# A three-stage transformer block on one NeuronCore: another product order and pinned transposes in the down projections

## The chip, the cores and the metric

The kernel runs on one NeuronCore of a Trainium2 chip. Its engines work side by side, each through its own list of instructions in order: PE (TensorE, matrix products and transposes), ACT (ScalarE), DVE (VectorE), POOL (GpSimd) and SP (SyncE, which here only issues DMAs). The metric is the device time of one execution in microseconds (us); lower is better.

## The reference

The layer has 1024 tokens of width 1024 and everything is float32:

```
x  = LN1(alpha*x + 0.5*SwiGLU_1(x))             # d_ff = 2816
x  = LN2(alpha*x + mixer(x))                    # GLA heads, and indexer -> top-256 keys -> attention
x  = LN3(alpha*x + 0.5*SwiGLU_2(x))
SwiGLU(x) = (silu(x @ Wg) * (x @ Wu)) @ Wd
LN(x) = (x - mean) * rsqrt(var + 1e-5) * g + b  # over the 1024 columns of a token
```

The mixer begins with one projection of x: a narrow one, m (the index key and gates, 112 columns), the four index queries iq (128 columns each), and then keys, values and the rest.

## The kernel before, in words

Every float32 product is made of three matmuls on pairs of fp32r tiles, a high part (`xh`, `whid`: a copy by ACT) and the rest (`xl`, `wlod`: a subtraction by DVE, L93 or L182).

A feed-forward stage is a "gate and up" part followed by `down`, here called Down 1 and Down 2. `down` multiplies 1024 x 2816 by 2816 x 1024 as seven half-size products (the scheme of Strassen in Winograd's form), in the order of the table `DOWN`: A11, A12, S4, S1, S2, S3, A22. Each product sums eleven tiles i = 0..10 into four PSUM banks `pd`, twelve matmuls a tile (L471), 132 a product; the last one adds to blocks 4 to 7. A tile is loaded by SP (`rd`, a half from `h_dram` and a half from the weights or their sums `t_dram`, L461 and L462) into a ring, and split by ACT (`whid`, L92) and DVE (`wlod`, L93). The results are added to eight blocks `acc` of 128 tokens each (L501 to L514), through the middle sum `u`, which is first the A11 product and becomes A11 + S2 (L506). Since S2 is the fifth product, the second halves of blocks 0 to 3 and both halves of blocks 4 to 7 get their part of `u` only then (L507, L518 and the next).

A block that is complete gets its layer norm: statistics (L207, L209, L211), POOL's power of -0.5 (`rs`, L193), then for most blocks DVE's `nb` (L221), ACT's scaling (L222), POOL's multiplication by g (L223) and DVE's addition of b (L224). Only blocks 4 to 7 of Down 2 take the other branch, `last`, on DVE alone (L215 over 1024 columns, L218 twice over 512). Blocks 0 to 3 are normed after the fifth product, blocks 4 to 7 after the last.

Down 1's blocks are transposed for the mixer by `split_T`: eight transposes a block on PE (L180) in two PSUM tiles `tp` of four, each of which ACT copies (`xh`, L181) and DVE subtracts from (`xl`, L182). `tp` has two buffers. Blocks 0 to 3 are transposed one each after i = 3, 4, 5, 6 of the last product; in that product PE's order is pinned by `in_order`, while ACT and DVE follow the scheduler's list. Then `index_parts` makes the mixer's first projections (`proj_feat`, L607 to L609, banks `pf` of two buffers) for tokens 0 to 511: m, evicted to `ik_hi`, `ik_lo` and `mT` (L640, L643, L644), and four iq (L651, L652), with the transposes of blocks 4 to 7 between them; then the same for tokens 512 to 1023. In between stand pieces of the index scores (`ps`, L682) and of the search for the top keys, which fill DVE in the mixer.

Of the kernel before, what the change touches and what calls it, by code (L numbers as in the profile page):

```python
# [111 lines left out]
class Block:  # L112
# [26 lines left out]
    def in_order(self):  # L139
# [6 lines left out]
        prev = None  # L146
        for i in body[start:]:
            if i.engine == mybir.EngineType.PE:
                if prev is not None:
                    self.tc.add_manual_dep(  # L150
                        i,
                        prev.name,
                        mybir.DependencyInfo(mybir.DependencyClass.NoSync, mybir.DependencyReason.DATA),
                        reason="in_order",
                    )
                prev = i
# [43 lines left out]
    def layer_norm(self, t, g_bc, b_bc, scale=1.0, last=False, st=None):  # L200
# [5 lines left out]
        for c in range(1 if made else 2):  # L206
            nc.vector.bn_stats(st[:, c, :], t[:, c * 512 : (c + 1) * 512])  # L207
# [6 lines left out]
        if last:  # L214
# [25 lines left out]
    DOWN = (("A11", "11"), ("A12", "21"), ("S4", "22"), ("S1", "T1"), ("S2", "T2"), ("S3", "T3"), ("A22", "T4"))  # L240
# [200 lines left out]
    def down(self, w_down, h_dram, t_dram, ps, load, after_block, after_all=None, ordered=None):  # L441
# [7 lines left out]
        last = len(self.DOWN) - 1  # L449

# [16 lines left out]
        def add(banks, r, i, hl):  # L467
            lh, ll = [x[:, r * P : (r + 1) * P] for x in hl]
            wh, wl = [x[:, HT:] for x in hl]
            for n, (left, right) in enumerate(((lh, wh), (lh, wl), (ll, wh))):  # L470
                nc.tensor.matmul(  # L471
                    banks[r], left, right, start=(i == 0 and n == 0), stop=(i == ng - 1 and n == 2)
                )

        ends = range(ng - (4 if ordered else RING), ng)
        done = list(range(4))
        acc = None
        for m in range(last + 1):
            pools = ((ps, "z"), (ps, "y")) if m % 2 == 0 else ((self.ps_tp, "tp"), (self.ps_pj, "pj"))
            banks = [pool.tile([P, 512], F32, tag=t, name=self.uid("pd"), bufs=2) for pool, t in pools for _ in range(2)]  # L480
            if m == last and ordered:
                ordered.enter_context(self.in_order())
            for i in range(ng if m < last else ends[0]):
                hl = prepare(m, i)
                for r in range(4):
                    add(banks, r, i, hl)
                if m == 0 and i == 2:
                    acc, u = load()
                    c11, c12 = [[acc[r][:, c * 512 : (c + 1) * 512] for r in range(4)] for c in range(2)]
                    c21, c22 = [[acc[4 + r][:, c * 512 : (c + 1) * 512] for r in range(4)] for c in range(2)]  # L490
                if m == last and after_all and i >= 3:
                    after_all(done.pop(0), acc)
            if m == last:
                made = [prepare(m, i) for i in ends]
            for r in range(4):
                p = banks[r]
                if m == 0:
                    nc.scalar.activation(u[r], p, AF.Copy)
                elif m in (1, 2):
                    c = (c11, c12)[m - 1][r]  # L500
                    V.scalar_tensor_tensor(c, c, 2.0 * ALPHA, p, ALU.mult, ALU.add)  # L501
                elif m == 3:
                    V.tensor_add(c12[r], c12[r], p)
                    V.scalar_tensor_tensor(c22[r], c22[r], 2.0 * ALPHA, p, ALU.mult, ALU.add)
                elif m == 4:
                    V.tensor_add(u[r], u[r], p)  # L506
                    V.tensor_add(c12[r], c12[r], u[r])  # L507
                elif m == 5:
                    V.tensor_add(c22[r], c22[r], p)
                    V.tensor_add(c21[r], c21[r], p)  # L510
                else:
                    for i, hl in zip(ends, made):
                        add(banks, r, i, hl)
                    V.tensor_add(c21[r], c21[r], p)  # L514
                    after_block(4 + r, acc, stats[r])
            if m == 1:
                for r in range(4):
                    V.tensor_add(c11[r], c11[r], u[r])  # L518
            elif m == 4:
                for r in range(4):  # L520
                    after_block(r, acc)
                    V.tensor_add(c22[r], c22[r], u[r])
                    V.scalar_tensor_tensor(c21[r], c21[r], 2.0 * ALPHA, u[r], ALU.mult, ALU.add)
            elif m == 5:
                stats = []
                for r in range(4):
                    stats.append(self.small.tile([P, 2, 6], F32, tag="st2", name=self.uid("st"), bufs=4))
                    V.bn_stats(stats[r][:, 1, :], c22[r])
        if after_all:
            for b in done:  # L530
                after_all(b, acc)
        return [(b, acc) for b in range(4, NB)]
# [94 lines left out]
    def index_parts(self, u, xT, ip, mT, between):  # L627
# [6 lines left out]
        for i in range(2):  # L634
# [9 lines left out]
            nc.scalar.activation(mT[64 : R_GA + 16, ts], pt[64 : R_GA + 16], AF.Copy)  # L644
            for t in range(4):
# [7 lines left out]
                if i == 0 and t:  # L653
# [425 lines left out]
    def run(self):  # L1079
# [80 lines left out]
        def back(n, ps, src, norm, after_block, *more):  # L1160

            kept, st = ExitStack(), ExitStack()
            pools = [
# [357 lines left out]
```

## Time and profile before

| | |
|---|---|
| median of 3 runs | 2080.42 us (2080.06 to 2080.82) |
| profiled execution | 2082.8 us, of which span 2081.0 us |
| granted clock of PE, mean | 0.974 |
| PE, DVE, ACT, POOL busy | 96%, 72%, 40%, 28% |
| Down 1, first `pd` matmul to the mixer's first projection | 453.67 to 677.52 us |
| index projections, first half of the tokens | 677.52 to 721.28 us |
| end of the span | 2081.0 us |

The rows further down give start and length of an instruction in us from the span's start, the engine, the line, the operation, what it writes and reads, and in brackets how long the engine had been idle and for what. The length of a PE row contains its pipeline: back to back, matmuls of 512 columns start about 0.23 us apart though each shows 0.39 us. [...]

### The profile page before, as it was taken

How to read it: one execution, taken by the hardware profiler on the slowest of the kernel's cores; microseconds unless marked ns; L12 is line 12 of the kernel's file. 1: busy time of each engine (PE TensorE's matmuls, PEld its weight loads, DVE VectorE, ACT ScalarE, POOL GpSimd, SP SyncE). 2: the span in 40 equal slices, each digit the busy share in tenths (PEclk: the TensorE clock that was granted, in tenths of full speed). 3: DMA queues.
4: the chain of work that ended last, by engine and by line, in shares of the span. 5: the costliest groups of instructions: out<-in, count | busy, mean ns of one | idle time of the engine just before them, and what ended most of it. 6: DMA issues, size and time to landing. Idle time of an engine off the chain costs nothing.

```text
span 2081.0 us, 26915 instructions
## 1 busy us (share of the span) xinstructions
PE 2004.6 (96%) x9752; PEld 1627.6 (78%) x9752; DVE 1500.3 (72%) x2378; ACT 836.1 (40%) x1330; POOL 591.6 (28%) x443
## 2 busy tenths in 40 slices
PE   8999999999998899899999899999999999999997
PEld 6888888888887688677777677787888888888885
DVE  5587787775578579999966455557587787775578
ACT  4323323334334344678544344423323323334332
POOL 3344454430003202133233000026354464420003
PEclk9999999999999999898998799999999999999999
DMA  5345445478655122011227521152345454478654
GB/s 172 112 152 188 138 163 169 142 253 291 201 179 182 61 91 86 17 54 57 53 85 169 147 72 36 52 189 75 123 154 179 142 174 150 145 273 274 201 184 151
DMA packets 192709, 298.44 MB, mean 143 GB/s; under 512 B 16304, under 2 KB 98368, under 8 KB 192576
## 3 DMA queue, kind: packets, MB, share of 16 engines
q1 hardware_dynamic: 192576, 296.72, 44.1%
q8 instruction: 77, 1.26, 0.3%
q14 instruction: 56, 0.46, 0.1%
HBM read 205.96 MB, written 90.70 MB: 143 GB/s over the span
## 4 chain that ended last, share of the span: by engine, by line
PE 73%; DVE 16%; issue 4%; DMA 3%; ACT 2%; POOL 1%; SPq 0%; POOLq 0%; DVEq 0%; ACTq 0%
PE pq L305 13%; PE pq L307 13%; PE pq L306 13%; PE pd L471 13%; DVE junk L732 3%; PE pv L1062 3%; PE tpe L1050 2%; PE pf L607 2%; PE pf L608 2%; DVE wlod L93 2%; PE pf L609 2%; PE pt L620 2%; PE pt L622 1%; PE pt L621 1%; DVE score L689 1%
## 5 line engine op out<-in xcount | busy, mean ns | idle before, releaser
L93 DVE TENSOR_TENSOR wloq<-rw,whiq 128x512 fp32r<-128x512 f32 (+1 forms) x208 | 213.8, 1030 | 110.9 <-ACT whiq L92 110.4
L93 DVE TENSOR_TENSOR wlod<-rd,whid 128x1024 fp32r<-128x1024 f32 x154 | 189.2, 1235 | 132.4 <-ACT whid L92 131.4
L92 ACT ACTIVATE whid<-rd 128x1024 fp32r<-128x1024 f32 x154 | 162.4, 1060 | 240.0 <-PE pd L471 145.8
L92 ACT ACTIVATE whiq<-rw 128x512 fp32r<-128x512 f32 (+1 forms) x208 | 163.5, 806 | 224.9 <-POOL rw L291 93.4
L471 PE MATMUL pd<-wlod,whid 128*128 128x512 f32 x616 | 240.9, 391 | 1.3 <-DVE wlod L93 1.1
L471 PE MATMUL pd<-whid,wlod 128*128 128x512 f32 x616 | 239.9, 390 | 0.0
L471 PE MATMUL pd<-whid 128*128 128x512 f32 x616 | 235.7, 392 | 0.5 <-ACT whid L92 0.5
L305 PE MATMUL pq<-b_h,whiq 128*128 128x512 f32 x576 | 229.2, 398 | 2.1 <-ACT b_h L92 2.1
L306 PE MATMUL pq<-b_l,whiq 128*128 128x512 f32 x576 | 225.7, 392 | 1.2 <-DVE b_l L93 1.2
L307 PE MATMUL pq<-b_h,wloq 128*128 128x512 f32 x576 | 225.6, 392 | 0.0
L193 POOL TENSOR_TENSOR rs<-ve,neghalf 128x1 f32<-128x1 f32 x24 | 23.9, 998 | 618.9 <-DVE ve L211 615.1
L417 ACT ACTIVATE c<-c 128x512 f32<-128x512 f32 x80 | 50.5, 632 | 238.8 <-DVE c L341 156.1
L620 PE MATMUL pt<-whi,xh 128*128 128x512 f32 x320 | 129.3, 405 | 9.2 <-ACT gg L1323 6.2
L305 PE MATMUL pq<-xh,whiq 128*128 128x512 f32 x352 | 137.9, 392 | 0.0
L471 PEld LDWEIGHTS pd<-wlod,whid 128*128 128x128 f32 x616 | 116.0, 188 | 27.4 <-DVE wlod L93 3.4
L307 PE MATMUL pq<-xh,wloq 128*128 128x512 f32 x352 | 137.2, 390 | 0.0
L306 PE MATMUL pq<-xl,whiq 128*128 128x512 f32 x352 | 137.1, 390 | 0.0
L471 PEld LDWEIGHTS pd<-whid 128*128 128x128 f32 x616 | 115.9, 188 | 25.4 <-ACT whid L92 1.8
L471 PEld LDWEIGHTS pd<-whid,wlod 128*128 128x128 f32 x616 | 116.0, 188 | 24.0
L305 PEld LDWEIGHTS pq<-b_h,whiq 128*128 128x128 f32 x576 | 108.9, 189 | 23.8 <-ACT b_h L92 2.7
L621 PE MATMUL pt<-wlo,xh 128*128 128x512 f32 x320 | 127.4, 398 | 0.0
L622 PE MATMUL pt<-whi,xl 128*128 128x512 f32 x320 | 127.2, 398 | 0.0
(262 smaller groups left out, 4592.9 us busy)
## 6 DMA issues: line engine op xcount, KB each, us to landing
rw<-in_ffn_w_gu_dram SPq DMA_DIRECT2D x88, 512.0 KB, 4.2
rd<-h_dram SPq DMA_DIRECT2D x154, 256.0 KB, 3.2
h_dram<-c SPq DMA_DIRECT2D x148, 256.0 KB, 3.1
rt<-in_ffn_w_down_dram SPq DMA_DIRECT2D x44, 512.0 KB, 3.4
t_dram<-rt SPq DMA_DIRECT2D x44, 512.0 KB, 3.0
rd<-t_dram SPq DMA_DIRECT2D x88, 256.0 KB, 3.1
rd<-in_ffn_w_down_dram SPq DMA_DIRECT2D x66, 256.0 KB, 4.3
raw<-in_w_in_dram SPq DMA_DIRECT2D x20, 512.0 KB, 3.8
```

The lines of the kernel that those rows point to most:

```text
L92: self.nc.scalar.activation(hi, src, AF.Copy)
L93: self.nc.vector.tensor_sub(lo, src, hi)
L305: mm(bank, wh[:, k, :], xh[:, k, :], start=(start and k == 0), stop=False)
L306: mm(bank, wh[:, k, :], xl[:, k, :], start=False, stop=False)
L307: mm(bank, wl[:, k, :], xh[:, k, :], start=False, stop=(stop and k == 3))
L417: nc.scalar.activation(t, t, AF.Silu)
L471: nc.tensor.matmul(banks[r], left, right, start=(i == 0 and n == 0), stop=(i == ng - 1 and n == 2))
L620: nc.tensor.matmul(pt, xh[:, k, cols], wh[:, k % 2, :], start=(k == 0), stop=False)
L621: nc.tensor.matmul(pt, xh[:, k, cols], wl[:, k % 2, :], start=False, stop=False)
L622: nc.tensor.matmul(pt, xl[:, k, cols], wh[:, k % 2, :], start=False, stop=(k == KD - 1))
L732: V.tensor_scalar(junk[:, :n], scores[b], thr, None, ALU.is_ge, ALU.add, accum_out=cnt)
L1062: nc.tensor.matmul(po[j * 64 : j * 64 + 64, q, :], v, ets[j][:, i, :], start=(kb == 0), stop=(kb == b))
```

## The change

`DOWN` becomes A11, S2, A12, S4, S1, S3, A22, so that `u` is complete after two products; S2's results and `u` go into the blocks from then on. In every product the first two and the last two tiles are grouped by bank (the last product: its last three in Down 1 and its last five in Down 2, where they were four and six), and a bank is evicted right after its group. Tiles are made two ahead of their use (`upto`). All layer norms of `down` take the branch on DVE alone; the statistics of the first half blocks are taken earlier. The transposes of blocks 0 to 3 come in halves, one tile `tp` after each of i = 1 to 7 and the eighth after i = 7 too, and in that stretch the order of ACT and of DVE is pinned as written. The norms of blocks 4 to 7 of Down 1 are no longer emitted after the last product but one by one in `index_parts`, before the transposes of the block before; the first is due after m's projection. The loads of `acc` are issued after tiles 0 and 1 instead of after tile 2.

```diff
-        if last:
+        if made:
             nc.vector.scalar_tensor_tensor(t, t, mv[:, 0:1], g_bc, ALU.subtract, ALU.mult)
             for c in range(2):
                 cs = slice(c * 512, (c + 1) * 512)
...
-    DOWN = (("A11", "11"), ("A12", "21"), ("S4", "22"), ("S1", "T1"), ("S2", "T2"), ("S3", "T3"), ("A22", "T4"))
+    DOWN = (("A11", "11"), ("S2", "T2"), ("A12", "21"), ("S4", "22"), ("S1", "T1"), ("S3", "T3"), ("A22", "T4"))
...
+        def upto(n):
+            while len(made) < min(n, len(self.DOWN) * ng):
+                made.append(prepare(*divmod(len(made), ng)))
...
+        def finish(name, r, p):
...
+            if name == "A11":
+                nc.scalar.activation(u[r], p, AF.Copy)
+                res(a1, p)
+            elif name == "S2":
+                inc(u[r], p)
+            elif name == "A12":
+                inc(a1, p)
+            elif name == "S4":
+                res(a2, p)
+            elif name == "S1":
+                inc(a2, p)
+                inc(b2, p)
+            elif name == "S3":
+                inc(b2, p)
+                inc(b1, p)
+            elif name == "A22":
+                inc(b1, p)
+                rest.append(lambda: (stat(4 + r, 0), after_block(4 + r, acc, stats[4 + r])))
+                if not ordered:
+                    rest.pop()()
+
+        def follow(name, r):
...
+            if name == "S2":
+                res(b1, u[r])
+                res(b2, u[r])
+            elif name == "A12":
+                stat(r, 0)
+            elif name == "S4":
+                inc(a2, u[r])
+            elif name == "S1":
+                stat(r, 1)
+                after_block(r, acc, stats[r])
+            elif name == "S3":
+                stat(4 + r, 1)
+
+        tail = 3 if ordered else 5
+        turns = [(b, k) for b in range(4) for k in (0, 4)] if after_all else []
...
+            ends = range(ng - (tail if m == last else 2), ng)
+            pinned = ExitStack()
             if m == last and ordered:
                 ordered.enter_context(self.in_order())
+                pinned.enter_context(self.in_order(mybir.EngineType.Activation, mybir.EngineType.DVE))
+            for grp in (range(0, 2), *([i] for i in range(2, ends[0])), ends):
+                upto(m * ng + grp[-1] + 3)
+                if grp is ends:
+                    while turns and m == last:
+                        after_all(*turns.pop(0), acc)
+                    pinned.close()
                 for r in range(4):
+                    for i in grp:
+                        add(out[r], r, m, i)
+                    if grp is ends:
+                        finish(name, r, out[r])
+                if m == last and turns:
+                    after_all(*turns.pop(0), acc)
+                if acc is None:
                     acc, u = load()
...
             nc.scalar.activation(mT[64 : R_GA + 16, ts], pt[64 : R_GA + 16], AF.Copy)
+            if i == 0:
+                next(between, None)
...
+                def turned():
+                    for b in range(4, NB):
+                        rest[b - 4]()
+                        if b > 4:
+                            self.split_T(acc[b - 1], b - 1, x1T)
+                        yield
+                    self.split_T(acc[b], b, x1T)
```

The same places of the instruction lists follow. First PE in Down 1's last product, where the transposes stand between tiles; the kernel before, around block 2:

```order
L471 MATMUL pd_5054<-wlod_5182,whid_5181 128x512
L471 MATMUL pd_5054<-whid_5181,wlod_5182 128x512
L180 MATMUL tp_5197<-ident,acc_2_3696 128x128 x4
L180 MATMUL tp_5204<-ident,acc_2_3696 128x128 x4
L471 MATMUL pd_5051<-whid_5214 128x512
L471 MATMUL pd_5051<-wlod_5215,whid_5214 128x512
```

A block's eight transposes stand together there, after a whole tile. In the changed kernel, around block 1, PE has:

```order
L477 MATMUL pd_5063<-whid_5074,wlod_5075 128x512
L180 MATMUL tp_5154<-ident,acc_1_3693 128x128 x4
L477 MATMUL pd_5060<-whid_5112 128x512
...
L477 MATMUL pd_5063<-whid_5112,wlod_5113 128x512
L180 MATMUL tp_5180<-ident,acc_1_3693 128x128 x4
L477 MATMUL pd_5060<-whid_5138 128x512
```

Eight transposes at a time became four, each followed by a tile.

ACT in the same stretch, the copies of tiles (`whid`) and of transposes (`xh`), in the kernel before:

```order
L92 ACTIVATE whid_5214<-rd_5211 128x1024
L92 ACTIVATE whid_5247<-rd_5244 128x1024
L92 ACTIVATE whid_5254<-rd_5251 128x1024
L92 ACTIVATE whid_5261<-rd_5258 128x1024
L181 ACTIVATE xh_3620<-tp_5131 128x4x128
L181 ACTIVATE xh_3620<-tp_5138 128x4x128
L92 ACTIVATE whid_5268<-rd_5265 128x1024
L181 ACTIVATE xh_3620<-tp_5164 128x4x128
```

The copies of four tiles stand ahead of block 0's first `xh`. In the changed kernel ACT has, from the first transposes on:

```order
L181 ACTIVATE xh_3620<-tp_5102 128x4x128
L92 ACTIVATE whid_5112<-rd_5109 128x1024
L181 ACTIVATE xh_3620<-tp_5128 128x4x128
L92 ACTIVATE whid_5138<-rd_5135 128x1024
L181 ACTIVATE xh_3620<-tp_5154 128x4x128
L92 ACTIVATE whid_5164<-rd_5161 128x1024
L181 ACTIVATE xh_3620<-tp_5180 128x4x128
L92 ACTIVATE whid_5190<-rd_5187 128x1024
```

Now one tile's copy stands between two `xh`, and DVE alternates `xl` and `wlod` in the same way.

DVE at the first index projections, with the norms' instructions (L207 to L224 before, L215 and L218 now) ahead of the evictions; the kernel before:

```order
L209 BN_AGGR mv_5364<-st_5049 128x2
L224 TENSOR_TENSOR acc_5_3699<-acc_5_3699,b_bc_3712 128x1024
L221 SCALAR_TENSOR_TENSOR nb_5344<-mv_5338,rs_5342 128x1
L211 TENSOR_SCALAR ve_5366<-mv_5364 128x1
L221 SCALAR_TENSOR_TENSOR nb_5370<-mv_5364,rs_5368 128x1
L224 TENSOR_TENSOR acc_6_3700<-acc_6_3700,b_bc_3712 128x1024
L224 TENSOR_TENSOR acc_7_3701<-acc_7_3701,b_bc_3712 128x1024
L643 TENSOR_TENSOR ik_lo<-pf_5459,ik_hi 64x512 x2
L652 SCALAR_TENSOR_TENSOR iq_5451<-pf_5489,iq_5451 64x512
L652 SCALAR_TENSOR_TENSOR iq_5452<-pf_5489,iq_5452 64x512
```

All four late norms stand ahead of m's eviction `ik_lo`. The changed kernel has on DVE:

```order
L218 SCALAR_TENSOR_TENSOR acc_4_3696<-acc_4_3696,rs_5437,b_bc_3710 128x512 x2
L673 TENSOR_TENSOR ik_lo<-pf_5402,ik_hi 64x512 x2
L211 TENSOR_SCALAR ve_5529<-mv_5527 128x1
L215 SCALAR_TENSOR_TENSOR acc_6_3698<-acc_6_3698,mv_5527,g_bc_3708 128x1024
L209 BN_AGGR mv_5581<-st_5058 128x2
L218 SCALAR_TENSOR_TENSOR acc_5_3697<-acc_5_3697,rs_5477,b_bc_3710 128x512 x2
L684 SCALAR_TENSOR_TENSOR iq_5394<-pf_5443,iq_5394 64x512
L182 TENSOR_TENSOR xl_3623<-tp_5483,xh_3622 128x4x128
L218 SCALAR_TENSOR_TENSOR acc_6_3698<-acc_6_3698,rs_5531,b_bc_3710 128x512 x2
L211 TENSOR_SCALAR ve_5583<-mv_5581 128x1
L182 TENSOR_TENSOR xl_3623<-tp_5490,xh_3622 128x4x128
L215 SCALAR_TENSOR_TENSOR acc_7_3699<-acc_7_3699,mv_5581,g_bc_3708 128x1024
```

Of the late norms only block 4's is complete there now (and block 5's first step L215 has been made); the others end among the evictions of m and the iq.

## Rows read from the trace of the kernel before

**Rows 1.** The page's part 1: busy time, share of the span, instructions.

```profile
PE 2004.6 (96%) x9752; PEld 1627.6 (78%) x9752; DVE 1500.3 (72%) x2378; ACT 836.1 (40%) x1330; POOL 591.6 (28%) x443
```

**Rows 2.** PE's waits between 440 and 760: engine, line, releaser, total us, times, longest.

```profile
PE tp L180 <- DVE xl L182: 8.1, 2, 7.7
PE ps L682 <- DVE iq L652: 7.9, 1, 7.9
PE pd L471 <- ACT whid L92: 0.2, 1, 0.2
```

**Rows 3.** Timeline of PE in Down 1's last product, blocks 0 and 1 transposed.

```profile
644.95 1.03 PE L180 MATMUL tp<-ident,acc 128*128 128x128 f32 x8
645.74 0.48 PE L471 MATMUL pd<-whid 128*128 128x512 f32 x1
...
656.47 1.97 PE L180 MATMUL tp<-ident,acc 128*128 128x128 f32 x8 [7.72 <-DVE xl L182]
```

**Rows 4.** Timeline of DVE in the same stretch.

```profile
635.12 3.42 DVE L224 TENSOR_TENSOR acc<-acc,b_bc 128x1024 f32<-128x1024 f32 x1
...
652.33 3.48 DVE L93 TENSOR_TENSOR wlod<-rd,whid 128x1024 fp32r<-128x1024 f32 x3
655.72 1.28 DVE L182 TENSOR_TENSOR xl<-tp,xh 128x512 fp32r<-128x512 f32 x2
```

**Rows 5.** Timeline of ACT in the same stretch.

```profile
651.88 1.06 ACT L92 ACTIVATE whid<-rd 128x1024 fp32r<-128x1024 f32 x1 [5.55 <-DVE wlod L93]
652.84 1.07 ACT L181 ACTIVATE xh<-tp 128x512 fp32r<-128x512 f32 x2
```

**Rows 6.** Timeline of PE in the index projections.

```profile
677.52 0.39 PE L607 MATMUL pf<-xh,whi 128*112 128x512 f32 x1
...
683.02 0.39 PE L607 MATMUL pf<-xh,whi 128*128 128x512 f32 x1
...
696.56 0.69 PE L682 MATMUL ps<-ik_hi,iq 128*128 128x384 f32 x1 [7.93 <-DVE iq L652]
...
698.21 0.63 PE L609 MATMUL pf<-xh,wlo 128*128 128x512 f32 x1
698.64 0.63 PE L607 MATMUL pf<-xh,whi 128*128 128x512 f32 x1
...
721.28 0.49 PE L607 MATMUL pf<-xh,whi 128*112 128x512 f32 x1
```

**Rows 7.** Timeline of DVE in the index projections.

```profile
690.13 4.48 DVE L224 TENSOR_TENSOR acc<-acc,b_bc 128x1024 f32<-128x1024 f32 x2 [2.80 <-POOL acc L223]
694.53 1.37 DVE L643 TENSOR_TENSOR ik_lo<-pf,ik_hi 64x512 fp32r<-64x512 f32 x2
```

**Rows 8.** Groups by shape: count | busy us, mean ns | idle before.

```profile
L224 DVE TENSOR_TENSOR acc<-acc,b_bc 128x1024 f32<-128x1024 f32 x12 | 20.9, 1751 | 2.8 <-POOL acc L223 2.8
...
L218 DVE SCALAR_TENSOR_TENSOR acc<-acc,rs,b_bc 128x512 f32<-128x512 f32 x8 | 5.6, 746 | 0.8 <-POOL rs L193 0.8
...
L215 DVE SCALAR_TENSOR_TENSOR acc<-acc,mv,g_bc 128x1024 f32<-128x1024 f32 x4 | 5.1, 1274 | 0.0
```

**Rows 9.** Windows: length, busy PE, PEld, DVE, ACT, POOL, clock, DMA share, GB/s.

```profile
696.50:701.30 4.80, 4.74 (x12) 3.87 (x13) 0.69 (x2) 0.62 (x2) 0.00 (x0) 0.50 0.11 38
...
845.00:970.00 125.00, 107.67 (x527) 83.78 (x526) 123.43 (x375) 95.37 (x171) 28.22 (x24) 0.89 0.11 32
...
2036.20:2068.80 32.60, 31.37 (x134) 24.44 (x132) 30.80 (x38) 8.34 (x8) 9.90 (x5) 1.00 0.43 143
```

**Rows 10.** Timeline of PE in Down 2's last product.

```profile
2050.81 0.50 PE L471 MATMUL pd<-wlod,whid 128*128 128x512 f32 x1 [0.46 <-DVE wlod L93]
...
2054.27 0.50 PE L471 MATMUL pd<-wlod,whid 128*128 128x512 f32 x1 [0.66 <-DVE wlod L93]
```

**Rows 11.** Timeline of DVE at the end of the program.

```profile
2068.95 0.67 DVE L514 TENSOR_TENSOR acc<-acc,pd 128x512 f32<-128x512 f32 x1
...
2076.42 1.41 DVE L218 SCALAR_TENSOR_TENSOR acc<-acc,rs,b_bc 128x512 f32<-128x512 f32 x2 [0.44 <-POOL rs L193]
```

More of the change, by code (lines that the diff above doesn't have):

```diff
@@ L449, in down @@
         last = len(self.DOWN) - 1
+        made = []
         def prepare(m, i):
@@ L465, in prepare, with add @@
             return hl
-        def add(banks, r, i, hl):
+        def upto(n):
+            while len(made) < min(n, len(self.DOWN) * ng):
+                made.append(prepare(*divmod(len(made), ng)))
+        def add(bank, r, m, i):
+            hl = made[m * ng + i]
             lh, ll = [x[:, r * P : (r + 1) * P] for x in hl]
@@ L470, in add @@
             for n, (left, right) in enumerate(((lh, wh), (lh, wl), (ll, wh))):
[L471 to L476, printed above, removed]
-        acc = None
-        for m in range(last + 1):
-            pools = ((ps, "z"), (ps, "y")) if m % 2 == 0 else ((self.ps_tp, "tp"), (self.ps_pj, "pj"))
-            banks = [pool.tile([P, 512], F32, tag=t, name=self.uid("pd"), bufs=2) for pool, t in pools for _ in range(2)]
+                nc.tensor.matmul(bank, left, right, start=(i == 0 and n == 0), stop=(i == ng - 1 and n == 2))
@@ new lines, in res, with inc, stat @@
+        def res(c, y):
+            V.scalar_tensor_tensor(c, c, 2.0 * ALPHA, y, ALU.mult, ALU.add)
+        def inc(c, y):
+            V.tensor_add(c, c, y)
+        def stat(b, c):
+            if b not in stats:
+                stats[b] = self.small.tile([P, 2, 6], F32, tag="stats", name=self.uid("st"), bufs=NB)
+            V.bn_stats(stats[b][:, c, :], acc[b][:, c * 512 : (c + 1) * 512])
+        def finish(name, r, p):
+            a1, a2 = [acc[r][:, c * 512 : (c + 1) * 512] for c in range(2)]
+            b1, b2 = [acc[4 + r][:, c * 512 : (c + 1) * 512] for c in range(2)]
+            if name == "A11":
[18 more added lines that the diff above has]
+                    rest.pop()()
@@ new lines, in follow @@
+        def follow(name, r):
+            a2 = acc[r][:, 512:]
+            b1, b2 = [acc[4 + r][:, c * 512 : (c + 1) * 512] for c in range(2)]
+            if name == "S2":
[10 more added lines that the diff above has]
+                stat(4 + r, 1)
@@ new lines, in down @@
+        tail = 3 if ordered else 5
+        turns = [(b, k) for b in range(4) for k in (0, 4)] if after_all else []
+        stats = {}
+        rest = []
+        acc = None
+        for m, (name, _) in enumerate(self.DOWN):
+            pools = ((self.ps_tp, "tp"), (self.ps_pj, "pj")) if m % 2 else ((ps, "z"), (ps, "y"))
+            out = [pool.tile([P, 512], F32, tag=t, name=self.uid("pd"), bufs=2) for pool, t in pools for _ in range(2)]
+            ends = range(ng - (tail if m == last else 2), ng)
+            pinned = ExitStack()
@@ L493, in down @@
-            if m == last:
-                made = [prepare(m, i) for i in ends]
-            for r in range(4):
[L496 to L528, printed above, removed]
@@ L536, in mixer_units @@
+            for r in range(4):
+                follow(name, r)
+        return rest, acc
     def mixer_units(self, w_in, w_out):
@@ L1459, in norm2 @@
             def norm2(b, acc, ln, st):
-                self.layer_norm(acc[b], *ln, scale=0.5, last=(b >= 4), st=st)
+                self.layer_norm(acc[b], *ln, scale=0.5, st=st)
                 for c in range(2):
```

54 lines of the change are left out of this document (21 added, 33 removed).

## The prediction

> **What bounds the kernel now.** I read the page's busy times first: PE works 2004.6 of 2081.0 us [rows 1], so a gain has to come from PE's idle time, from stretches at the lower clock, or from what follows PE's last instruction. Next PE's waits around Down 1, which the change touches most [rows 2]: two of them, 7.7 and 7.9 us, hold nearly all there is. Then the timelines of the three engines at each of the two.
>
> The first stands in Down 1's last product. PE turned block 0 at 644.95 and wanted to turn block 1 at 648.7, but began at 656.47, 7.72 us late, for the `xl` that frees the two PSUM tiles [rows 3]. DVE made those `xl` at 655.72, after three `wlod` in a row [rows 4]; ACT made their `xh` at 652.84, behind a `whid` that had itself waited 5.55 us for a buffer that a `wlod` frees [rows 5]. Nothing was slow for its size; the tiles' splits stood in front of the transposes' on both engines, and DVE was late, with additions and norms of the product before (one L224 took 3.42 us [rows 4], against 1.75 in the mean [rows 8]).
>
> The second stands in the index projections: PE waited 7.93 us, until 696.56, for an `iq` eviction on DVE [rows 6]. DVE was in the last two L224 from 690.13 to 694.6, after 2.80 us of waiting for POOL, and only then came m's `ik_lo` [rows 7], which stands behind all four late norms in DVE's list.
>
> After the second wait PE ran at the lower level for a while: a granted clock of 0.50 from 696.5 to 701.3, with 12 matmuls in 4.8 us [rows 9]. At the upper level they need 12 x 0.229 us, from the 24 matmuls between 677.52 and 683.02 [rows 6]. So a stall of that length costs 4.8 - 2.75 = 2.05 us beyond itself. After the first stall eight transposes took 1.97 instead of 1.03 us [rows 3], the same halving; I count 2.0 there too.
>
> **The change, part by part.** The sums go against the profiled execution, whose span is 2081.0 us and whose time 2082.8; the median of the runs is 2080.42, so 2.4 lower.
>
> *Half blocks and pinned order.* In the steps between i = 1 and i = 7, PE has four transposes and twelve matmuls: 0.4 us (half of 645.74 - 644.95 [rows 3]) and 12 x 0.229 = 2.75, so 3.15 us a step. ACT's share is one `xh` of 0.53 and one `whid` of 1.06 [rows 5], DVE's one `xl` of 0.64 and one `wlod` of 1.16 [rows 4]: 1.6 and 1.8 us, with room. The pinned chain of a step, transposes, `xh`, `whid`, `wlod`, is 0.7 + 0.53 + 1.06 + 1.16, so 3.45 us (0.7, my estimate for the way from the first transpose to `xh`, is a little under the 0.79 us that eight take). That is longer than a step, but the tile is needed two steps later, so about 2.9 us are spare. Each half has a PSUM tile of its own and the next half that wants it comes two steps later as well. So 7.7 + 2.0 go. What is late next is the end of the pinned stretch: seventh and eighth half come together and the last tile's `wlod` stands behind them, and it is needed by the first bank's third tile soon after. I put 0 to 2 us there and take 0.7: **-9.0**.
>
> *Earlier additions, norms on DVE alone.* `u` is complete after the second product. Of blocks 0 to 3 the fifth product then leaves two additions, one statistic and the norm each, where it left four adding steps, two statistics and the norm, and the norms have the whole sixth product to be ready. A norm costs DVE L215 and two L218, 1.27 + 1.49 = 2.77 us, in place of L224's 1.75 [rows 8] and `nb`: up to 1 us more, twelve times. This is hidden under PE in the sixth product (about 30 us, 132 x 0.229) for eight of the twelve; without the cover it would be 1 us each. The late four of Down 1 are in the next item, of Down 2's late four nothing changes. **0**.
>
> *Late norms among the projections.* m's `ik_lo` now waits for block 4's norm and a first step of block 5's, not for four norms and POOL. By DVE's list from the last bank on (additions, statistics, weights' `wlo`, L215 of blocks 4 and 5, L218 of block 4) at these durations, `ik_lo` is done some 10 us after PE starts m's projection; two projections last 2 x 5.5 = 11 us [rows 6]. After them come block 4's transposes, which need that norm and have it; but ACT's `mT` stands behind the first `xh` of block 4, and the third projection needs m's bank. That is a new wait of about 1.2 us; bounds 0 and 3 (three norm steps behind one another). Queued behind `mT` on ACT are block 4's second `xh` and the next `iq`, for which nobody waits for another 5 us. The 7.93 and 2.05 go, 1.2 comes: **-8.8**.
>
> *Starts of the two Downs.* PE waited 0.2 us for a `whid` at the end of Down 1's first product [rows 2], behind a load that SP issues after eight loads of `acc`. The loads of `acc` go two tiles earlier, in front of two tiles' loads instead of one. Bounds: a gain of 0.5 each, and a loss of 3 each if SP's queue lets the tiles through late; around Down 1 PE waited for no `whid` longer than 0.2 us [rows 2], so I take **-0.4** for both.
>
> *Down 2's last product.* There PE waited 0.46 and 0.66 us for `wlod` [rows 10], and from 2036.2 to 2068.8 it needed 32.6 us for 132 matmuls [rows 9], or 30.2 at 0.229: 2.4 us too many. DVE was busy 30.80 of the 32.6, with blocks 0 to 3 on it; these are out of the way now. Between 0 and 2.4, I take **-2.0**.
>
> *The end.* The last bank's addition begins at 2068.95, and the last L218 ends at 2076.42 + 1.41 [rows 11], 8.9 us later, because four norms of some 3.9 us on DVE queue there. Five tiles at the end put the banks 15 x 0.229 = 3.4 us apart instead of 4.1, which alone would make the queue longer by 2 us; but before, the banks started late, behind the waits above. Bounds +2 and -3; I take **-1.0**.
>
> Sum: -9.0 - 8.8 - 0.4 - 2.0 - 1.0 = -21.2, of the profiled span 2081.0 to 2059.8; against the median, 2080.42 - 21.2 = 2059.2. I say **2059 us**.
>
> **The rivals.** *The second wait stays (2068).* If DVE's list still delays `iq` and `ik_lo` by much, the second stall keeps its price, 8.8. For it: the norms are longer on DVE, and six of their steps still stand among the evictions. Against it: no POOL stands between them any more, and m's eviction moved ahead of the last three L218 pairs.
>
> *The mixer gives it back (2067).* From 845 to 970 DVE is busy 123.43 of 125 us and PE idles 17.3 [rows 9], so there DVE decides. If the pieces of search and projections fall otherwise, half of that idle time, 8 us, may come or go. For it: their order moves a little in the changed kernel. Against it: DVE reaches that stretch earlier by the same 18 us, since it begins with scores that PE makes earlier, and the work in it is the same.
>
> *Slower: the pinned order keeps PE at half clock (2086).* Every one of the eight half-block steps ties PE to ACT and DVE. If the chain of 3.45 us had to fit into the step of 3.15, PE would wait 0.3 us in each. The trace shows that waits of 0.46 and 0.66 us left the granted clock at 1.00 [rows 9, 10], but not what eight in a row do. If they cost the clock for the whole product, 132 matmuls start 0.43 us apart, from 698.21 to 698.64 [rows 6], instead of 0.229: +26.5, so 2059 + 26.5 = 2086, slower than before. This decides from the point at which a tile is wanted in the step after its making instead of the second after; the list has it two ahead. [...]
>
> *The change doesn't do what it says.* The lists show it does: halves between tiles, `xh` and `whid` in turn, norms among the projections. What is left of this is a load or a PSUM bank that holds PE in each of seven products by the new grouping; at 2 us in each it eats 14 of the 21 (2073).
>
> **How the numbers follow.** The forecast's chance is 0.60, with an own range of 2052 to 2065: the bounds above, added as they would seldom all fall together, give about 7 below and 6 above. The second wait staying 0.14, the mixer giving back 0.12, the grouping's waits 0.07, the slower one 0.07. Range 2047 to 2071: up to the two rivals at 2067 and 2068 with some of their own spread, down to a mixer that gives 8 us more and an end that is shorter; 2073 and 2086 are left out. A measurement of this kernel can tell a difference of 0.2%, 4.2 us, from none. Faster than 2076.2: the forecast, and nearly all of the three milder rivals, 0.91. Within 0.2%: 0.03. Slower: 0.06.
>
> **What would show it.** In the changed profile PE's `tp` wait of 7.7 us and its `ps` wait of 7.9 us should be gone, the granted clock should be 1.00 in Down 1's last product, and that product should take about 34 us with its transposes. m's projection of the second half of the tokens, at 721.28 before [rows 6], should begin at 702 to 704. From there to the end of the mixer the kernel should run as before, only earlier. Down 2's last product should take about 30.5 us, and the last L218 should end under 9 us after the last bank. I am wrong if `tp` still waits for `xl` between tiles, if the third projection waits over 3 us, or if less of the gain at that point is left when Down 2 begins.

## The result and the profile after

The changed kernel takes 2061.48 us in the median of 6 runs (2058.09 to 2065.96); the kernel before took 2080.43 us (2079.27 to 2082.52) beside it. The ratio is 0.991 with a 95% interval of 0.9897 to 0.9922, a gain of 19 us. The forecast was 2059.

The rows below are of one profiled execution: 2063.2 us, span 2061.4. PE's line of the page, to be held against [rows 1]:

```profile
PE 1995.9 (97%) x9752; PEld 1620.4 (79%) x9752; DVE 1495.7 (73%) x2390; ACT 820.9 (40%) x1318; POOL 569.7 (28%) x431
```

PE's instructions are as many as before; of the 19.6 us that the span is shorter, 8.7 are busy and 10.9 idle time. PE's waits from 440 to 760 us, the answer to [rows 2]:

```profile
PE pf L637 <- ACT mT L674: 0.9, 1, 0.9
PE pd L477 <- DVE wlod L93: 0.8, 1, 0.8
PE pf L638 <- DVE xl L182: 0.5, 1, 0.5
```

The waits of 7.7 and 7.9 us are gone. The first two that are left are the two new ones that the prediction had priced, at 1.2 and 0.7. Two steps of Down 1's last product, on PE, ACT and DVE in turn (timelines, as [rows 3 to 5]):

```profile
642.76 0.60 PE L180 MATMUL tp<-ident,acc 128*128 128x128 f32 x4
645.95 0.60 PE L180 MATMUL tp<-ident,acc 128*128 128x128 f32 x4
...
643.40 0.60 ACT L181 ACTIVATE xh<-tp 128x512 fp32r<-128x512 f32 x1 [1.65 <-PE tp L180]
643.89 1.05 ACT L92 ACTIVATE whid<-rd 128x1024 fp32r<-128x1024 f32 x1
...
644.03 0.69 DVE L182 TENSOR_TENSOR xl<-tp,xh 128x512 fp32r<-128x512 f32 x1 [1.02 <-ACT xh L181]
644.97 1.23 DVE L93 TENSOR_TENSOR wlod<-rd,whid 128x1024 fp32r<-128x1024 f32 x1 [0.26 <-ACT whid L92]
```

A step is 645.95 - 642.76 = 3.19 us; from its first transpose to the end of `wlod` are 644.97 + 1.23 - 642.76 = 3.44 us, as the prediction worked out (3.15 and 3.45; the expectations of two runs below put the chain at 3.35). Now it is ACT and DVE that wait, each in every step. Windows of that product and of the index projections (length, busy PE, PEld, DVE, ACT, POOL, granted clock as a share of full speed, DMA share, GB/s):

```profile
634.00:668.90 34.90, 34.14 (x166) 27.94 (x165) 25.41 (x32) 15.31 (x20) 0.96 (x1) 1.00 0.57 163
668.90:702.40 33.50, 32.60 (x161) 26.86 (x159) 26.04 (x42) 11.70 (x20) 4.92 (x5) 1.00 0.28 95
```

The clock is 1.00 throughout. In the index projections, the third one after its wait and the second half's m on PE, and m's eviction on DVE with the norm step that follows it ([rows 6, 7]):

```profile
681.78 0.50 PE L637 MATMUL pf<-xh,whi 128*128 128x512 f32 x1 [0.90 <-ACT mT L674]
...
702.45 0.49 PE L637 MATMUL pf<-xh,whi 128*112 128x512 f32 x1
...
678.29 1.38 DVE L673 TENSOR_TENSOR ik_lo<-pf,ik_hi 64x512 fp32r<-64x512 f32 x2
...
679.77 1.28 DVE L215 SCALAR_TENSOR_TENSOR acc<-acc,mv,g_bc 128x1024 f32<-128x1024 f32 x1
```

`ik_lo` ends at 679.7, about 16 us earlier than at 694.53 + 1.37 before, and the second half's m begins at 702.45 instead of 721.28. At the end of the program, on DVE ([rows 11]), the first bank's addition, the last bank's and the last norm step:

```profile
2040.79 0.69 DVE L483 TENSOR_TENSOR acc<-acc,pd 128x512 f32<-128x512 f32 x1 [4.94 <-PE pd L477]
...
2052.15 0.68 DVE L483 TENSOR_TENSOR acc<-acc,pd 128x512 f32<-128x512 f32 x1
...
2056.82 1.41 DVE L218 SCALAR_TENSOR_TENSOR acc<-acc,rs,b_bc 128x512 f32<-128x512 f32 x2 [0.44 <-POOL rs L193]
```

The last matmul begins at 2049.43 and the last bank's addition 2.7 us after it, behind steps of the norms before it in DVE's list; in the kernel before it came 0.45 us after (2068.50 and 2068.95).

To compare kernels I cut each profiled execution by starts of PE rows: Down 1 from its first `pd` to the first projection; the index projections from there to the second half's m; "between" from there to Down 2's first `pd`; Down 2 to its last `pd`; the end from there to the end of DVE's last instruction. The first column is the median of the timed runs, the others are of one profiled execution; all is in us, and the experiments that the names stand for follow below.

| kernel | median | Down 1 | index | between | Down 2 | end |
|---|---|---|---|---|---|---|
| before | 2080.43 | 223.85 | 43.76 | 1134.66 | 212.56 | 9.33 |
| changed | 2061.48 | 214.80 | 33.55 | 1136.73 | 210.25 | 8.80 |
| b_order | 2083.61 | 219.58 | 44.27 | 1141.70 | 210.28 | 8.50 |
| b_dve_norm | 2084.13 | 218.01 | 40.07 | 1143.77 | 209.55 | 13.56 |
| e_frame | 2072.68 | 217.59 | 33.82 | 1141.50 | 212.82 | 8.80 |
| e_old_order | 2071.70 | 214.47 | 33.55 | 1143.11 | 210.13 | 11.98 |
| e_pool_norm | 2066.75 | 214.64 | 33.86 | 1139.87 | 209.80 | 8.81 |
| e_both | 2068.42 | 214.28 | 33.84 | 1142.48 | 210.24 | 8.81 |
| e_free | 2062.66 | 213.20 | 32.30 | 1137.37 | 209.62 | 8.82 |
| e_whole | 2057.41 | 213.49 | 33.95 | 1131.71 | 210.08 | 8.81 |
| e_one_ahead | 2064.49 | 216.24 | 33.55 | 1138.68 | 209.39 | 8.81 |
| e_none_ahead (1 run) | 2086.15 | 238.61 | 33.55 | 1136.91 | 209.31 | 8.80 |
| f_whole6 | 2054.27 | 213.16 | 33.96 | 1130.84 | 210.28 | 6.85 |
| f_free6 | 2061.44 | 213.88 | 32.30 | 1139.96 | 210.11 | 6.86 |

The change against before: Down 1 -9.05, index -10.21, between +2.07, Down 2 -2.31, end -0.53; the parts ahead of Down 1 +0.43. The sum is -19.6, the difference of the spans.

### The profile page after: what moved, and what is told of

It reads as the page before. It is cut to its first block, busy times and chain, and to the rows that moved or that the text cites. A ratio compares the mean times of both kernels' runs of the same rounds, so it can differ in the third digit from the quotient of the medians.

```text
span 2061.4 us, 26913 instructions
## 1 busy us (share of the span) xinstructions
PE 1995.9 (97%) x9752; PEld 1620.4 (79%) x9752; DVE 1495.7 (73%) x2390; ACT 820.9 (40%) x1318; POOL 569.7 (28%) x431
## 4 chain that ended last, share of the span: by engine, by line
PE 73%; DVE 12%; DMA 5%; issue 5%; POOL 3%; ACT 2%; SPq 0%; POOLq 0%; DVEq 0%; ACTq 0%
PE pd L477 17%; PE pq L306 12%; PE pq L305 12%; PE pq L307 12%; DVE junk L764 3%; PE pv L1094 3%; PE tpe L1082 2%; PE pf L637 2%; PE pf L638 2%; PE pf L639 2%; DMA rd<-in_ffn_w_down_dram 2%; PE pt L650 2%; PE pt L651 1%; DVE score L721 1%; PE pt L652 1%
## 5 line engine op out<-in xcount | busy, mean ns | idle before, releaser
L193 POOL TENSOR_TENSOR rs<-ve,neghalf 128x1 f32<-128x1 f32 x24 | 35.0, 1456 | 629.6 <-DVE ve L211 629.6
```

## The experiments

My theory was the prediction's: the lists' order made the first stall, and the pinned half blocks cure it; POOL and the place of the late norms made the second. The rival was DVE's load: whatever makes DVE early enough cures both.

**Parts undone, one at a time.** The first takes the pinning of ACT and DVE out:

```diff
-                pinned.enter_context(self.in_order(mybir.EngineType.Activation, mybir.EngineType.DVE))
```

> The changed kernel with ACT and DVE no longer pinned in Down 1's last product (PE stays pinned, halves stay). The scheduler then puts the copies of four tiles ahead of the first xh and two wlod ahead of the first xl. Theory 'list': the order of the two engines' lists made the 7.7 us stall, so PE waits 3 to 8 us for xl again and the half clock follows: 2066 to 2071 us. Rival 'load': DVE was late with additions and norms and is light now, so no tp wait over 1 us comes back: 2060 to 2063 us.

The rival holds, as far as pinning goes; the halves stay in this kernel. ACT and DVE then work as follows (timelines of ACT, DVE, and PE's transposes):

```profile
639.11 1.04 ACT L92 ACTIVATE whid<-rd 128x1024 fp32r<-128x1024 f32 x1
640.06 0.58 ACT L181 ACTIVATE xh<-tp 128x512 fp32r<-128x512 f32 x1
...
640.49 2.35 DVE L93 TENSOR_TENSOR wlod<-rd,whid 128x1024 fp32r<-128x1024 f32 x2
642.75 0.69 DVE L182 TENSOR_TENSOR xl<-tp,xh 128x512 fp32r<-128x512 f32 x1
...
638.63 0.60 PE L180 MATMUL tp<-ident,acc 128*128 128x128 f32 x4
641.83 0.60 PE L180 MATMUL tp<-ident,acc 128*128 128x128 f32 x4
645.01 0.60 PE L180 MATMUL tp<-ident,acc 128*128 128x128 f32 x4
```

Tiles' splits stand in front of the transposes' again, two `wlod` ahead of the first `xl`, but `xl` is done at 643.4 and its PSUM tile is wanted at 645.01. No wait is left in Down 1 or in the index projections, which even gain 1.6 and 1.25 us on the pinned kernel: the tile at the end is made earlier, and `mT` stands ahead of `xh`. The total is not lower (2062.66 against 2061.48): the differences of "between", discussed in the next section, are larger than this gain.

The second transposes whole blocks again, pinned:

```diff
-        turns = [(b, k) for b in range(4) for k in (0, 4)] if after_all else []
+        turns = [(b, 0) for b in range(4)] if after_all else []
...
-                if m == last and turns:
+                if m == last and turns and grp[-1] >= 3:
```

> The changed kernel with blocks 0 to 3 transposed whole again, eight transposes after i = 3, 4, 5 and 6, with everything else as changed, the pinned order too. Theory 'halves': both PSUM tiles are taken at once, so PE waits for xl before each next block, 1 us or more in all; Down 1 (first pd matmul to the first projection, 223.9 us before, 214.8 changed) takes 216 to 222 us. Rival 'load': with DVE light the two xl are done some 2.4 us after the first transpose and the next block comes 3.5 us after it, so no wait: Down 1 takes 213 to 215 us. The mixer's list changes with every variant, so its length may differ by 5 us; the total is 2058 to 2067 us.

No `tp` wait there either, and Down 1 takes 213.49 us. With tiles two ahead and a light DVE, halves are not needed where the order is pinned, nor pinning where there are halves; a kernel without both was not run. The total is 4 us lower than the change's; "between" alone is 5.0 lower.

The third puts S2 back to the fifth place, with the additions that this asks for:

```diff
-    DOWN = (("A11", "11"), ("S2", "T2"), ("A12", "21"), ("S4", "22"), ("S1", "T1"), ("S3", "T3"), ("A22", "T4"))
+    DOWN = (("A11", "11"), ("A12", "21"), ("S4", "22"), ("S1", "T1"), ("S2", "T2"), ("S3", "T3"), ("A22", "T4"))
```

> The changed kernel with the product order of before (S2 fifth), so that the fifth product leaves eight more DVE instructions of 0.6 us and the norms begin some 5 us later; halves, pinned order, grouping and norms on DVE stay. Theory 'list': the pinned order alone keeps the transposes moving, no tp wait over 1 us, 2061 to 2063 us. Rival 'load': DVE is late again in the last product, PE waits 2 to 8 us there, 2064 to 2071 us. In Down 2, where nothing is pinned, 'load' gives back about 1 to 2 us.

Down 1, index and Down 2 stay as changed, as by the theory "list"; the total is outside of its range all the same, by 6.4 us of "between" and 3.2 at the end. I had not expected either, and a verdict by the total would have gone wrong.

The fourth and fifth bring the norms of before back: with ACT and POOL, and then also emitted right after the last product.

```diff
-        if made:
+        if made and dve:
...
-            self.layer_norm(acc[b], *ln, scale=0.5, st=st)
+            self.layer_norm(acc[b], *ln, scale=0.5, st=st, dve=False)
```

> The changed kernel with the norm of before (nb, ACT scaling, POOL times g, DVE plus b) for Down 1's eight blocks and Down 2's blocks 0 to 3; where they are emitted stays as changed. Theory 'path': the second stall came from POOL's 2.9 us in front of each of DVE's last additions, so block 4's transposes and the iq evictions come late and PE waits 4 us or more between 675 and 692: 2065 to 2070 us. Rival 'place': it went because the norms are emitted among the projections; waits there stay under 1.5 us, 2061 to 2063 us.

> The changed kernel with both parts of the late norms as before: nb, ACT, POOL and DVE, and emitted right after the last product instead of among the projections. Theory 'place or path': either one cures the second stall, and without both it is back: the index projections (first to second m projection, 43.8 us before, 33.6 changed) take 38 to 44 us. Rival 'end of the product': the stall went because the last product no longer ends late on DVE, and the list puts ik_lo ahead of the norms by itself: 33 to 35 us. The total is 2060 to 2066 us by the rival, 2066 to 2076 by the theory.

The index projections take 33.86 and 33.84 us: curing the second stall needs neither part. Both totals lie where the theory that failed had put them; only the stages tell. The two kernels have the same instructions in the same order on all five engines but for one small DVE instruction ahead of Down 1; the scheduler undoes where the norms are emitted. So their "between", 1139.87 and 1142.48, and their medians, 2066.75 and 2068.42, also say what one list varies by.

**One part alone, on the kernel before.** First all norms of both Downs on DVE alone, shown here for Down 1:

```diff
-            self.layer_norm(acc[b], *ln, scale=0.5, st=st)
+            self.layer_norm(acc[b], *ln, scale=0.5, last=True, st=st)
```

> The kernel before with one part of the change: all norms of the two Downs on DVE alone. Theory 'POOL': DVE was late in Down 1 because its additions of b waited for POOL or ran long beside it (3.4 us for one of 1.75 in the mean); the tp wait of 7.7 us falls under 3 and Down 1 takes 215 to 219 us; in the index projections no POOL stands ahead of ik_lo, 36 to 40 us for 43.8; total 2066 to 2074 us. Rival 'list': DVE's work grows by 1 us a norm, the splits still stand ahead of the transposes, Down 1 takes 222 to 226 us; total 2076 to 2083 us.

> The kernel before with one part of the change: S2 second, with the additions that this asks for; norms, transposes and grouping as before. Theory 'load': eight additions fewer on DVE at the fifth product let the norms and the sixth product's additions end earlier, and the tp wait falls under 3 us: Down 1 takes 215 to 219 us, and the index projections stay at 42 to 45; total 2069 to 2077 us. Rival 'list': the four copies still stand ahead of block 0's xh, Down 1 takes 221 to 224 us; total 2077 to 2083 us.

(b_order has the edit of `DOWN` above in the other direction, with its additions.) PE's waits from 440 to 760, of b_dve_norm and then of b_order:

```profile
PE ps L682 <- DVE iq L652: 4.1, 1, 4.1
PE tp L180 <- DVE xl L182: 3.2, 2, 2.8
```

```profile
PE ps L685 <- DVE iq L655: 7.9, 1, 7.9
PE tp L180 <- DVE xl L182: 3.5, 2, 3.2
```

Each part alone takes more than half of the first wait (b_order's 3.2 us is a little more than I had set): Down 1 gains 5.8 and 4.3 us. In b_order the splits stand ahead of the transposes as before, ten tiles of the last product in front of block 0's `xh` and `xl`; in b_dve_norm nine, so a part of its gain may be the list's. Norms on DVE alone also lighten DVE, against the prediction's price of up to 1 us more for each. DVE's groups by shape from 600 to 656, the norms of blocks 0 to 3, before and in b_dve_norm:

```profile
L224 DVE TENSOR_TENSOR acc<-acc,b_bc 128x1024 f32<-128x1024 f32 x4 | 7.0, 1760 | 0.0
L221 DVE SCALAR_TENSOR_TENSOR nb<-mv,rs 128x1 f32<-128x1 f32 x4 | 5.0, 1246 | 0.0
```

```profile
L218 DVE SCALAR_TENSOR_TENSOR acc<-acc,rs,b_bc 128x512 f32<-128x512 f32 x8 | 5.7, 754 | 0.0
L215 DVE SCALAR_TENSOR_TENSOR acc<-acc,mv,g_bc 128x1024 f32<-128x1024 f32 x4 | 5.1, 1282 | 0.0
```

Its statistics apart, a norm took 3.0 us of DVE before and takes 2.7 here: `nb`, on 128x1 values, was as dear in the mean as a pass over the block (the rows of e_frame below show why). The norms without POOL also halve the second wait. Yet both kernels are some 4 us slower than the kernel before beside them, 2079.75 us (ratios 1.002, 1.0011 to 1.0029, and 1.0016, 1.0006 to 1.0025): "between" grows by 9.1 and 7.0 us, the end of b_dve_norm by 4.2. Neither total was in a range that I had given.

**The frame alone.** Old order, old norms, old place; what stays is the tiles two ahead, the grouping by bank, the shorter last group, halves and pinning, and also the earlier statistics and loads of `acc`.

```diff
-    DOWN = (("A11", "11"), ("S2", "T2"), ("A12", "21"), ("S4", "22"), ("S1", "T1"), ("S3", "T3"), ("A22", "T4"))
+    DOWN = (("A11", "11"), ("A12", "21"), ("S4", "22"), ("S1", "T1"), ("S2", "T2"), ("S3", "T3"), ("A22", "T4"))
...
-        if made:
+        if made and dve:
```

> The changed kernel without its three parts that touch DVE's load and the late norms: old product order, norms by nb, ACT, POOL and DVE, late norms emitted right after the last product. What stays is the frame: tiles two ahead, grouping and eviction by bank, three tiles at the end, half blocks, pinned ACT and DVE. Theory 'frame': it is what cures both stalls, Down 1 takes 214 to 216 us (223.9 before, 214.8 changed) and the index projections 33 to 35. Rival 'load': the pinned order needs one of the two cuts of DVE's load; without both, xl stands behind late additions and norms, Down 1 takes 218 to 224 us, the index projections 33 to 35 all the same, because the list has ik_lo ahead of the last additions of b.

Down 1 lies between the two forecasts, with 217.59 us: 6.3 of the 9.05 that the change gains there. The longest wait left in it, and the one in Down 2's last product:

```profile
PE tp L180 <- DVE xl L182: 1.5, 1, 1.5
PE pd L477 <- DVE wlod L93: 2.0, 2, 1.4
```

The index projections have nearly their full gain. DVE and POOL there:

```profile
678.42 1.38 DVE L670 TENSOR_TENSOR ik_lo<-pf,ik_hi 64x512 fp32r<-64x512 f32 x2 [0.83 <-ACT ik_hi L667]
679.83 0.15 DVE L211 TENSOR_SCALAR ve<-mv 128x1 f32<-128x1 f32 x1
679.90 2.24 DVE L221 SCALAR_TENSOR_TENSOR nb<-mv,rs 128x1 f32<-128x1 f32 x1
...
682.16 1.23 DVE L224 TENSOR_TENSOR acc<-acc,b_bc 128x1024 f32<-128x1024 f32 x1
...
685.92 3.41 DVE L224 TENSOR_TENSOR acc<-acc,b_bc 128x1024 f32<-128x1024 f32 x1
```

```profile
679.74 2.39 POOL L223 TENSOR_TENSOR acc<-acc,g_bc 128x1024 f32<-128x1024 f32 x1 [1.25 <-ACT acc L222]
...
683.50 8.08 POOL L223 TENSOR_TENSOR acc<-acc,g_bc 128x1024 f32<-128x1024 f32 x3 [0.86 <-ACT acc L222]
```

POOL is as slow as ever (2.39 us for one L223 and 8.08 for three; 3.16 for one and 4.66 for two at this place in the kernel before), but the list has `ik_lo` in front of all four L224, at the time it had in the changed kernel. Beside POOL's multiplications one L224 takes 3.41 instead of 1.23 us, and an instruction on 128x1 values 2.24 instead of 0.15.

**The clock under short waits**, the prediction's slower rival. Tiles one ahead and none ahead in the last product:

```diff
-                upto(m * ng + grp[-1] + 3)
+                upto(m * ng + grp[-1] + (2 if m == last and ordered else 3))
```

> The changed kernel with the tiles of Down 1's last product made one step ahead of their use instead of two. The prediction's slower rival: the chain of 3.45 us does not fit into a step of 3.15, PE waits 0.3 us or more in each of seven steps, and the clock falls to half for the product: 2063 us from the waits alone, 2087 with the clock. From the changed kernel's trace: whid and wlod end 3.35 us after the step's first transpose, and the next step's second matmul wants wlod 3.19 + 0.4 + 0.2 = 3.8 us after it, so there is no wait and 2060 to 2063 us.

> The changed kernel with the tiles of Down 1's last product made in the step that uses them. The chain from the first transpose to the end of wlod, 3.35 us in the changed trace, then stands before the step's second matmul, which would come 0.4 + 0.2 us after the transposes: PE waits about 2.5 us in each of seven steps, 17 us, and a little more at the ends. The prediction's slower rival had the clock fall to half under such waits: another 20 us and more, 2100 us and above, granted clock near 0.5 to 0.6 in the product. If the clock stays at 1.00 between waits of 2.5 us, 2078 to 2082 us.

One ahead still fits (Down 1 +1.4 us, no wait in the steps between half blocks, a granted clock of 1.00 from 634.0 to 668.9): `wlod` is wanted by the next step's second matmul, not by its transposes, which the prediction's comparison of 3.45 with 3.15 us had left out. With none ahead (1 instead of 2 in the edit; one run only), PE's waits from 630 to 700, windows of 3 us after the second wait of the first three steps, and two matmuls of the first step:

```profile
PE pd L477 <- ACT whid L92: 11.0, 7, 1.6
PE pd L477 <- DVE wlod L93: 5.6, 9, 0.8
```

```profile
642.40:645.40 3.00, 3.00 (x7) 2.42 (x8) 0.00 (x0) 0.00 (x0) 0.00 (x0) 0.50 0.56 175
650.00:653.00 3.00, 3.00 (x14) 2.45 (x15) 0.00 (x0) 0.00 (x0) 0.00 (x0) 1.00 0.48 175
656.20:659.20 3.00, 3.00 (x7) 2.42 (x8) 0.00 (x0) 0.00 (x0) 0.00 (x0) 0.50 0.57 175
```

```profile
643.39 0.63 PE L477 MATMUL pd<-whid 128*128 128x512 f32 x1
643.81 0.63 PE L477 MATMUL pd<-wlod,whid 128*128 128x512 f32 x1
```

PE waits 1.6 and then 0.8 us in each step, and the granted clock goes down to 0.50 in the first, third and fifth of seven steps, for about 3 us each time, and stays at 1.00 in the others (the fifth is read from matmuls that start 0.43 us apart from 670.42 to 672.56; the clock from 660.0 to 665.0, in the fourth, was 1.00, and in the last two the matmuls start 0.23 us apart again). Down 1 grows by 23.8 us, of which 15.8 are more waiting. The clock's share I count from the starts of matmuls: 22 of them come 0.43 us or so after the one before instead of 0.23, about 4.6 us in all. The rest are matmuls around each wait that start later than the wait's own figure holds. So the clock did fall under these waits, as the rival had it, at under a fifth of its 26.5 us.

**A better version.** On two variants, e_whole (whole blocks, pinned) and e_free (half blocks, not pinned), Down 2 gets six tiles at the end and a pinned PE order there:

```diff
-        tail = 3 if ordered else 5
+        tail = 3 if ordered else 6
...
+            if m == last and not ordered:
+                straight.enter_context(self.in_order())
```

> The variant with whole blocks, and in Down 2 six tiles at the end instead of five with PE's order pinned there; the lists up to Down 2's last product are the same. The banks are then 18 x 0.227 = 4.1 us apart, more than the 3.9 us of one norm on DVE, so the queue of norms does not build up: from the last matmul to the last L218's end 6.2 us instead of 8.8, total 2054 to 2056 us. Rival: the sixth tile comes late (its buffer comes free only with the fifth tile's matmuls), PE waits 1 to 3 us at the start of the group, and the total stays at 2057.

> The variant with half blocks but ACT and DVE not pinned, with the same six tiles at the end of Down 2. Its lists up to there are those of the unpinned variant (2062.7 us). The same theory: 2.6 us less, 2059 to 2061 us; by the rival it stays at 2062.5.

Both ends shrink by 1.96 us, less than the 2.6 forecast. DVE at the end of f_whole6, where the last matmul begins at 2042.12:

```profile
2030.31 0.69 DVE L483 TENSOR_TENSOR acc<-acc,pd 128x512 f32<-128x512 f32 x1 [1.76 <-PE pd L477]
...
2042.88 0.68 DVE L483 TENSOR_TENSOR acc<-acc,pd 128x512 f32<-128x512 f32 x1
2043.48 1.41 DVE L218 SCALAR_TENSOR_TENSOR acc<-acc,rs,b_bc 128x512 f32<-128x512 f32 x2
...
2047.56 1.41 DVE L218 SCALAR_TENSOR_TENSOR acc<-acc,rs,b_bc 128x512 f32<-128x512 f32 x2 [0.44 <-POOL rs L193]
```

Only block 6's L218 still stands behind the last addition. From the first bank's addition to the last matmul are 11.8 us now, and were 8.6 in the changed kernel, where PE's order at the end was left to the scheduler. How much is the sixth tile's and how much the pinned order's was not tried apart. f_whole6 takes 2054.27 us (2053.93 to 2055.20), 0.9881 of before (0.9866 to 0.9896): the fastest here, 7 us under the change, of which some 2 are this end and most of the rest is "between", which nobody planned. f_free6 is 1.2 us under e_free in the median, by runs that spread over 7 us, and its 2061.44 misses the forecast of 2059 to 2061.

## Why the prediction was right, and where it was not

*The sum.* Forecast -21.2, measured -19.6 in the profiled executions. Down 1 with its start: -9.2 forecast, -9.05 measured. Index: -8.8 and -10.2. Down 2 with its start: -2.2 and -2.3. The end: -1.0 and -0.5. Not in the sum: +2.1 between, which the mixer rival had allowed for, and +0.4 ahead of Down 1. That the total came within 1.6 us is partly luck: the index gained 1.4 more than forecast, and "between" took 2.1.

*The first stall: right in size, wrong in what cures it.* The step on half blocks and pinned order said that the order of the lists let the stall go. e_free and e_whole show that neither pinning nor halves are needed while the other stays, b_order and b_dve_norm that either cut of DVE's load alone takes more than half of the wait, and e_frame, where both cuts are missing, that the rest of the change gives 6.3 of 9.05 us without them. The parts overlap: each alone gives half or more, the frame with either cut gives all. I had written of DVE that it "was late, with additions and norms of the product before", and then priced the cuts at 0, with up to 1 us more for each norm, where a norm of blocks 0 to 3 got 0.3 us cheaper on DVE. In Down 2 they are all that there is: e_frame's Down 2 takes 212.82 us, as before, and waits 2.0 us for `wlod` in its last product. Either cut does it (e_old_order 210.13, e_pool_norm 209.80).

*The second stall: right in size, wrong in its cause.* "Late norms among the projections" credited POOL's absence and the place of emission. e_both has neither and loses nothing; the list itself puts `ik_lo` ahead of all late L224 as soon as the frame is there. POOL's share is real only on the kernel before (3.7 us in b_dve_norm). Pinning, halves and the tiles two ahead in the last product are not what turns the list: each was taken out, with the late norms as changed, and the index projections stayed at 32.3 to 34.0 us (e_free, e_whole, e_none_ahead). Of the rest of the frame (grouping, three tiles at the end, tiles two ahead in the other products, earlier loads) nothing was tried apart, and it stays open. The gain is also 1.4 us over the forecast: PE's busy time in the stretch fell by 2.8 us (35.38 to 32.60), where I had put 2.05 on the clock, and its idle time by 7.5, where I had 6.7. The stretch in the kernel before:

```profile
677.52:721.28 43.76, 35.38 (x161) 28.50 (x159) 24.15 (x34) 15.68 (x25) 10.98 (x37) 0.88 0.22 72
```

*New waits.* 0.7 and 1.2 us were forecast for the pinned stretch's end and for `mT`; 0.76 and 0.90 came, at these places.

*The slower rival* did not come, for the reason given: tiles are two ahead. It did not come at one ahead either, so its deciding point was set wrongly.

*The mixer rival* was mis-sized. I gave it 0.12 and 8 us. Over the fourteen kernels "between" runs from 1130.8 to 1143.8 us, though none of them edits that part. Here are windows over the mixer's middle, from the last index score to the last GLA output (the same stretch of the program), of e_whole and of b_dve_norm:

```profile
838.60:1139.70 301.10, 271.30 (x1496) 214.52 (x1494) 237.57 (x611) 187.52 (x360) 91.28 (x70) 0.90 0.28 79
```

```profile
848.70:1161.30 312.60, 278.03 (x1497) 220.64 (x1495) 242.14 (x611) 187.24 (x360) 92.53 (x70) 0.88 0.27 76
```

The same work takes 11.5 us longer, with 4.8 us more of idle PE and a clock of 0.88 instead of 0.90. The scheduler lists this stretch anew for most kernels. Where the list there is the same, "between" differs by 0.9 (e_whole, f_whole6) and 2.6 us (e_free, f_free6; e_pool_norm, e_both and, with the same order there, e_frame); otherwise by up to 13. One execution is not much to go by: timed runs of one kernel spread by up to 8.3 us (e_old_order). But if I take from each "between" how far its execution lay from its kernel's median, kernels with one list agree within 1.3 us, and all still run from 1131 to 1144. So the list decides most of it. For the change this way of counting gives +2.7 instead of +2.1, which none of its parts explains. Which piece of the list does it stays open.

## What to carry to other kernels

When one engine is late into a stretch, its order there may be only where the lateness shows: price the cuts of its load from rows of that stretch, and try the pinned order and the lighter engine apart. Where a scheduler lists the program, an edit moves stretches that it does not touch, here by up to 13 us against a gain of 19; compare kernels stage by stage, and measure that spread before a total decides. Look in the changed list for what an edit of emission order did: the place of the late norms did nothing here.

## What the runs showed of the hardware

After a wait of 3.18 us in b_order PE's next eight transposes took 1.97 us, as after 7.72 us before [rows 3], against 1.04 for the next eight. The granted clock was 0.50 over these 1.97 us in both kernels. After a wait of 2.83 us in b_dve_norm eight transposes took 1.88 us; after one of 1.52 us in e_frame the granted clock stayed at 1.00 (634.0 to 672.0). It was 1.00 too in the kernel before from 677.52 to 683.02, where the prediction counts 0.229 us a matmul. The rows of b_order, and its window:

```profile
651.68 1.97 PE L180 MATMUL tp<-ident,acc 128*128 128x128 f32 x8 [3.18 <-DVE xl L182]
658.18 1.04 PE L180 MATMUL tp<-ident,acc 128*128 128x128 f32 x8
```

```profile
651.68:653.65 1.97, 1.97 (x9) 1.97 (x10) 1.86 (x3) 0.60 (x1) 0.00 (x0) 0.50 1.08 203
```

Waits of 1.6 and 0.8 us in turn, in e_none_ahead, lowered the granted clock to 0.50 in three of seven steps and left it at 1.00 in the others.
